# A streaming encoder step on one core: both feed-forwards begin with two blocks taken by quarter

## The chip, the cores and the metric

The kernel runs on one core of one Trainium2 chip. The metric is device time in microseconds (us). Before the change three runs took 2466.3, 2466.51 and 2468.87, with the median at 2466.51.

A core has five engines with queues of their own: PE (TensorE: products and transposes; its weight loads are listed as PEld), DVE (VectorE), ACT (ScalarE), POOL (GpSimd) and SP (SyncE, which here issues most loads and stores). Engines wait for one another by semaphores. Products accumulate in banks of the PSUM memory (512 columns of f32 each), which VectorE and ScalarE read.

## The reference

One step of a macaron encoder: half a SwiGLU feed-forward, an in-projection, attention and a recurrence side by side, a gated merge, an out-projection, half a feed-forward, and a last norm. All activations and weights are f32, D = 1024, D_FF = 2816.

```
def half_ffn(x, g, w_gate, w_up, w_down):
    h = rmsnorm(x, g)
    return x + 0.5 * ((silu(h @ w_gate) * (h @ w_up)) @ w_down)

x = half_ffn(x, ffn1_norm, ffn1_w_gate, ffn1_w_up, ffn1_w_down)
qa, ka, va, zf, ih, qh, g, ga, gb = split(rmsnorm(x, mix_norm) @ w_in)
...
merged = sigmoid(ga + b) * (oa @ w_branch_a) + sigmoid(gb + b) * (ob @ w_branch_b)
x = x + merged @ w_out
x = half_ffn(x, ffn2_norm, ffn2_w_gate, ffn2_w_up, ffn2_w_down)
y = rmsnorm(x, final_norm)
```

oa is the stick-breaking attention's output, ob that of the HGRN2 recurrence. There are 1072 token columns: 16 meta tokens, 1024 prompt frames and 32 sample frames. The outputs are y, the new K and V rows and the recurrence's states.

## The kernel before

**Layout.** Activations lie feature-major: 128 features on the partitions, 8 k-tiles for D, token columns along the free dimension. An f32 operand is split in a high and a low half (ScalarE copies the high one, VectorE subtracts to get the low one, `split` at L219 and L220; `weights` does it for a loaded block at L202 and L203). A product of one k-tile is three matmuls: high by high, high by low, low by high (L103 in the profile, where every matmul is recorded; transposes are L106). A product of four k-tiles by 268 columns is thus 12 matmuls, called a half product below.

**Feed-forwards.** The columns are cut in four quarters of 268 (264 in FFN2), two halves `b` by two halves `th`. Blocks of 128 hidden features come in units of two. The class `Seven` computes each unit by a seven-product scheme (Strassen) on 2 by 2 blocks of operands; the scheme needs the sums T1 to T4 of operand quarters, which `sums(b)` makes on VectorE. Blocks 0 and 1 are not done in this way: `plain` takes them as ordinary products, so that PE has work while the operands and sums are made. Before, `plain(0)` goes over all four quarters for the gate and the up weights of block 0, then `plain(1)` for block 1; `rest` follows with units 1 to 10. Their results go through `mid_dram` to the down projection, a list of jobs of seven products p1 to p7 that `run` interleaves: p6 and p7 of a job stand inside the next job.

**FFN1's start.** The token rows are loaded in row tiles of 128 (`xt`) with leftovers of 12 rows per quarter (`odds`). For a quarter, ScalarE takes square sums, a chain of small VectorE operations and one POOL power gives the row scales (L790 to L796), POOL writes them on a diagonal (L804, L807), PE spreads them over the partitions by a product with ones, ScalarE copies that to `R`, and `columns` turns the rows by transposes, scales them (L836) and splits them. All rows are asked for ahead of the weights. The sums of both halves stand between `plain(0)` and `plain(1)`.

**Merge.** `merge(m)` for block m loads two gates (`ga`, `gb`, L1633), multiplies the two branch products by them (L1641) and splits the sum into `mh`, `ml`. `out_block` adds out-projections into `acc`, which starts as the residual (three loads, L1624, issued ahead of the first gates). The blocks go in groups (0, 1), (2, 3), (4) and (5, 6, 7); the last group goes over three column tiles of 384, 384 and 288, and behind each tile `squares` takes its square sums (L1661, L1662), a product with ones adds them up, and `operands` scales and splits the tile for FFN2 (L1693).

**What sets the order.** A scheduler orders each engine's instructions from their dependences, except where `PE.on` keeps PE in the order of the code, and where a dependence is added by hand. `bank(rotate=True)` hands out PSUM banks in turn; the tags are mm, z, tr and o.

Of the kernel before, what the change touches and what calls it, by code (L numbers as in the profile page):

```python
# [82 lines left out]
def tile_encoder_step(ctx, tc, x_prompt, x_sample, cache_k, cache_v, state_hgrn, meta_tokens,  # L83
# [101 lines left out]
    def weights(parts, own=None):  # L185
        raw = wp.tile([P, D], F32, tag="raw", name="raw", bufs=2)
        n = 0
        for src, k in parts:
# [13 lines left out]
        A.activation(hi, raw, AF.Copy)  # L202
        V.tensor_tensor(lo, raw, hi.bitcast(F32), op=ALU.subtract)  # L203
# [14 lines left out]
    def split(dst_h, dst_l, src):  # L218
        A.activation(dst_h, src, AF.Copy)  # L219
        V.tensor_tensor(dst_l, src, dst_h.bitcast(F32), op=ALU.subtract)  # L220
# [50 lines left out]

    def finish_one():
        while waiting:
            waiting.pop(0)()
# [54 lines left out]
    class Seven:  # L329
# [60 lines left out]
        def plain(self, c, before=lambda q: None, after=lambda q: None):  # L390

            qw, where = self.qw, self.where
            gw = self.ahead.pop(c) if c in self.ahead else self.block(self.w_gate, c)
            uw = self.block(self.w_up, c)
            g = self.tile("g", [P, T])
            for q in range(4):
                before(q)
                b, th = divmod(q, 2)
                pss = []
                for wh, wl in (gw, uw):  # L400
                    ps = bank(rotate=True)
                    for kh in range(2):
                        ks = slice(kh * 512, (kh + 1) * 512)
                        product(ps, (wh[:, ks], wl[:, ks]), self.B[kh, th, b], kh == 0)
                    pss.append(ps)
                after(q)
                silu(where(g, th, b), pss[0][:, :qw])
                V.tensor_tensor(where(g, th, b), pss[1][:, :qw], where(g, th, b), op=ALU.mult)
            self.gs.append(g)
# [164 lines left out]
        def down(self, w, resid, final, after, early):  # L574
# [70 lines left out]
            def run(jobs):  # L645
# [9 lines left out]
                for job in jobs:  # L655
                    step(job.p1)
                    if before:
                        step(before.p6)
                    step(job.p2)
                    step(job.p4 if job.done == "end" else job.p3)  # L660
                    if before:
                        step(before.p7)
                        if before.done:
                            queue += before.done()
                            every[0] = max(1, 20 // len(queue))
                    step(job.p3 if job.done == "end" else job.p4)
                    if job.done == "end":
# [3 lines left out]
                if before.done != "end":  # L671
                    before.p6()
                before.p7()
# [68 lines left out]
    with tc.tile_pool(name="f1", bufs=2) as pool:  # L742
# [21 lines left out]
        G.memset(odds, 0.0)  # L764
        rows = []
        for q in range(4):
            for h in range(2):
                tag, n = (("g", 4), ("g", 4), ("raw2", 2), ("S", 2))[q]
                xt = pool.tile([P, D], F32, tag=tag, name="xt", bufs=n)
                load(xt, 0, q * QW + h * P, P)  # L770
                rows.append(xt)
            if q == 0:
                for x in range(4):
                    load(odds, 32 * x, x * QW + 2 * P, ODD)
# [3 lines left out]
        functions("silu_and_others")  # L778

        def scales(tiles):  # L780
            m = len(tiles)
            ss = pool.tile([P, 3, 4], F32, tag="ss", name="ss", bufs=4)
            V.memset(ss, 1.0)
            for j, xt in enumerate(tiles):
                for h in range(2):
                    junk = temp(pool, "junk")
                    A.activation(junk.bitcast(BF16)[:, :512], xt[:, h * 512:(h + 1) * 512], AF.Square,
                                 accum_out=ss[:, h, j:j + 1])
            ms, y, r1 = ss[:, 0, :m], ss[:, 1, :m], ss[:, 2, :m]
            V.tensor_tensor(ms, ms, y, op=ALU.add)  # L790
            V.tensor_scalar(ms, ms, 1.0 / D, EPS, op0=ALU.mult, op1=ALU.add)
# [1064 lines left out]
```

## Time and profile before

| | us |
|---|---|
| median of three runs | 2466.51 |
| the profiled execution | 2468.0 |
| its span in the profile | 2466.2 |
| PE busy | 2396.0 |
| VectorE busy | 1669.0 |
| ScalarE busy | 1017.8 |
| POOL busy | 257.1 |

The span is the profiled execution from its first to its last instruction. A group of instructions is given as line, engine, operation, output <- input, then the count; `[... <-X]` is the idle time ahead of an instruction and who ended it. The name of the output is that of the tile in the code: `ps_z` is a bank with the tag z. PEclk is the clock granted to TensorE, 1.00 being full. PE's busy time includes stretches at half of it.

### The profile page before, as it was taken

What the parts mean: (1) busy time and instruction counts of PE and PEld (TensorE: products, weight loads), DVE (VectorE), ACT (ScalarE), POOL (GpSimd) and SP (SyncE); (2) the same over time, 40 slices, a digit from 0 to 9 for tenths busy, and PEclk for the clock granted to TensorE, in tenths of its full rate; (3) what the DMA queues carried; (4) which work ended last, traced back from release to release, by engine and by line L of the source; (5) the groups of instructions that cost most, each with busy time, mean ns of one, the idle gap of its engine ahead of it and who ended that gap; (6) DMA issues with size and microseconds to landing.
All of it is one profiled execution on the core that took longest, in us unless ns stands there. A gap on an engine that the chain in (4) does not pass through costs nothing.

```text
span 2466.2 us, 47916 instructions
## 1 busy us (share of the span) xinstructions
PE 2396.0 (97%) x19500; PEld 2292.9 (93%) x19500; DVE 1669.0 (68%) x3144; ACT 1017.8 (41%) x2129; POOL 257.1 (10%) x461
## 2 busy tenths in 40 slices
PE   6999999999999999999999999999799999999997
PEld 5999999989999998899888888999799999999997
DVE  4866676767766477764666665556966767676876
ACT  6444444442225233332445544323444444453223
POOL 1011010100003012121000000112011111110000
PEclk9999999999999999999999999999899999999999
DMA  7334343487652111111211122522234444468761
GB/s 199 106 127 164 124 168 123 160 315 280 244 211 79 50 44 48 57 48 50 59 45 45 49 67 62 193 87 100 75 130 150 140 150 141 152 239 323 272 237 72
DMA packets 270371, 331.93 MB, mean 135 GB/s; under 512 B 41078, under 2 KB 228726, under 8 KB 264518
## 3 DMA queue, kind: packets, MB, share of 16 engines
q1 hardware_dynamic: 247942, 244.96, 29.7%
q0 software_dynamic: 22208, 83.91, 9.0%
q8 instruction: 153, 2.51, 0.4%
q14 instruction: 68, 0.56, 0.1%
HBM read 213.93 MB, written 114.89 MB: 133 GB/s over the span
## 4 chain that ended last, share of the span: by engine, by line
PE 84%; DVE 5%; issue 5%; DMA 4%; ACT 2%; POOL 1%; SPq 0%; DVEq 0%; ACTq 0%; POOLq 0%
PE ps_mm L103 28%; PE ps_z L103 26%; PE ps_o L103 9%; PE pu L103 6%; PE ps_tr L103 5%; PE pf L103 4%; PE pv L103 4%; PE ps_tr L106 2%; DMA mid_dram<-st 1%; DMA raw<-in_ffn_w_down_dram 1%; PE ps_z L106 1%; DMA u_xl<-mid_dram 1%; DVE wlo L203 1%; POOL mid_dram L371 1%; PE ps_mm L106 0%
## 5 line engine op out<-in xcount | busy, mean ns | idle before, releaser
L103 PE MATMUL ps_mm<-xh,whi 128*128 128x384 f32 (+2 forms) x960 | 320.0, 334 | 0.5 <-DVE raw L1487 0.5
L103 PE MATMUL ps_mm<-xh,wlo 128*128 128x384 f32 (+2 forms) x960 | 313.2, 326 | 0.0
L103 PE MATMUL ps_mm<-xl,whi 128*128 128x384 f32 (+2 forms) x960 | 312.8, 326 | 0.0
L219 ACT ACTIVATE whi<-S 128x1024 fp32r<-128x1024 f32 x122 | 129.3, 1059 | 311.3 <-PE ps_z L103 135.7
L371 POOL DMA_DIRECT2D mid_dram<-st x150 | 104.3, 706 | 830.4 <-DVE st L220 805.5
L103 PEld LDWEIGHTS ps_mm<-xh,whi 128*128 128x128 f32 x960 | 181.1, 189 | 9.1 <-issue 5.0
L103 PEld LDWEIGHTS ps_mm<-xl,whi 128*128 128x128 f32 x960 | 181.0, 189 | 1.2
L103 PEld LDWEIGHTS ps_mm<-xh,wlo 128*128 128x128 f32 x960 | 181.2, 189 | 0.3
L220 DVE TENSOR_TENSOR wlo<-S,whi 128x1024 fp32r<-128x1024 f32 x122 | 149.1, 1222 | 34.3 <-ACT whi L219 31.4
L220 DVE TENSOR_TENSOR st<-g,st 128x536 fp32r<-128x536 f32 (+1 forms) x150 | 104.7, 710 | 85.8 <-ACT st L219 85.8
L202 ACT ACTIVATE whi<-raw 128x1024 fp32r<-128x1024 f32 x67 | 70.4, 1056 | 180.9 <-PE ps_mm L103 139.1
L1279 DVE TENSOR_TENSOR_SCAN left<-left,oneb 128x512 f32<-128x512 f32 (+6 forms) x112 | 107.4, 959 | 54.8 <-ACT left L119 54.2
L220 DVE TENSOR_TENSOR wlo<-raw,whi 128x1024 fp32r<-128x1024 f32 x80 | 76.6, 957 | 75.4 <-ACT whi L219 73.6
L219 ACT ACTIVATE st<-g 128x536 fp32r<-128x536 f32 (+1 forms) x150 | 94.5, 643 | 79.4 <-DMA mid_dram<-st 63.8
L103 PE MATMUL ps_z<-acc1s,whi 128*128 128x268 f32 (+1 forms) x480 | 106.3, 285 | 0.0
L103 PE MATMUL ps_z<-xh1s,whi 128*128 128x268 f32 (+1 forms) x360 | 102.8, 286 | 0.0
L103 PE MATMUL ps_z<-xl1s,whi 128*128 128x268 f32 (+1 forms) x360 | 102.6, 285 | 0.0
L103 PE MATMUL ps_z<-xh1s,wlo 128*128 128x268 f32 (+1 forms) x360 | 102.6, 285 | 0.0
L103 PE MATMUL ps_z<-xh2s,whi 128*128 128x268 f32 (+1 forms) x352 | 100.4, 285 | 0.0
L103 PE MATMUL ps_z<-xl2s,whi 128*128 128x268 f32 (+1 forms) x352 | 100.3, 285 | 0.0
L103 PE MATMUL ps_z<-xh2s,wlo 128*128 128x268 f32 (+1 forms) x352 | 100.1, 285 | 0.0
L203 DVE TENSOR_TENSOR wlo<-raw,whi 128x1024 fp32r<-128x1024 f32 x67 | 82.8, 1241 | 25.1 <-ACT whi L202 21.3
(715 smaller groups left out, 7603.8 us busy)
## 6 DMA issues: line engine op xcount, KB each, us to landing
mid_dram<-st POOLq DMA_DIRECT2D x75, 536.0 KB, 3.9
mid_dram<-st POOLq DMA_DIRECT2D x75, 528.0 KB, 4.0
raw<-in_ffn_w_gate_dram SPq DMA_DIRECT2D x44, 512.0 KB, 3.7
raw<-in_ffn_w_up_dram SPq DMA_DIRECT2D x44, 512.0 KB, 3.8
raw<-in_w_in_dram SPq DMA_DIRECT2D x44, 512.0 KB, 3.7
raw<-in_ffn_w_down_dram SPq DMA_DIRECT2D x40, 512.0 KB, 6.1
u_xl<-mid_dram SPq DMA_DIRECT2D x8, 1608.0 KB, 6.6
u_xh<-mid_dram SPq DMA_DIRECT2D x8, 1608.0 KB, 10.8
```

The lines of the kernel that those rows point to most:

```text
L103: return self.queue(nc.tensor.matmul(*args, **more))
L106: return self.queue(nc.tensor.transpose(*args, **more))
L202: A.activation(hi, raw, AF.Copy)
L203: V.tensor_tensor(lo, raw, hi.bitcast(F32), op=ALU.subtract)
L219: A.activation(dst_h, src, AF.Copy)
L220: V.tensor_tensor(dst_l, src, dst_h.bitcast(F32), op=ALU.subtract)
L371: nc.gpsimd.dma_start(self.mids[i, :, :, NAMES.index(name)], st.bitcast(F32))
L1279: V.tensor_tensor_scan(rev(st[:rows]), rev(st[:rows]), one, 1.0 if carry is None else carry[:rows], op0=ALU.mult, op1=ALU.mult)
```

## The change

1. *FFN1's start.* The leftovers follow the first two row tiles, then four weight blocks (gate and up of blocks 0 and 1), then the other rows. Products of a zero tile `busy` are put ahead of the first transposes (18), ahead of the first spread (6) and ahead of the first real product (5). A square sum is one operation over 1024 columns. The first quarter's scale chain and diagonal are VectorE's alone but for the power; the later ones are POOL's. `first_columns` turns seven k-tiles into seven banks at once and splits them two at a time.
2. *`plain((0, 1))`.* Both blocks together, quarter by quarter: four fixed banks (mm, mm, tr, o) take gate and up of blocks 0 and 1, first for the lower four k-tiles, then for the upper four. After each half product a callback `step(q, j)` may put in work for the next quarter (transposes, spread) and the sums, which now stand inside quarters 1 and 3. The same in FFN2.
3. `lmax` and `causalb` on VectorE are held back behind a mark.
4. *Merge's start.* `merge` is now the class `Merge`. One residual tile is loaded ahead of the gates of blocks 0 and 1, two behind them.
5. *Out-projections.* The groups are (0, 1), (2, 3), (4, 5); inside a tile four banks take one block after another.
6. *Merge's end.* Blocks 6 and 7 go tile by tile: both merge products of tile j, then the product with ones and the scaling for tile j - 1, then the out-projection of tile j, then its square sums. `operands` is a list of pieces which are put in one at a time, between out-projections of tile 1 and inside FFN2's first quarters.
7. *Down projections.* One job more (`tight`) has all of its seven products done before the next job begins.

PE at the merge's end, around the product with ones (`cst`) that adds up the square sums of the second column tile (`t_ga` before, `ga` and `gb` after); `mh` and `ml` are a merged block's halves, `whi`, `wlo` and `raw_...` those of weights, `xh_17813` the branch outputs of the third tile. Before:

```order
L103 MATMUL ps_mm<-mh,raw_19293 128x288
L103 MATMUL ps_mm<-ml,raw_19293 128x288
L103 MATMUL ps_mm<-mh,raw_19294 128x288
L103 MATMUL ps_z<-t_ga,cst 128x384 x2
L103 MATMUL ps_tr<-mh,whi 128x288
L103 MATMUL ps_tr<-ml,whi 128x288
L103 MATMUL ps_tr<-mh,wlo 128x288
```

After:

```order
L103 MATMUL ps_o<-mh,raw_19174 128x384
L103 MATMUL ps_o<-ml,raw_19174 128x384
L103 MATMUL ps_o<-mh,raw_19175 128x384
L103 MATMUL ps_z<-xh_17813,whi 128x288
...
L103 MATMUL ps_mm<-xh_17813,wlo 128x288
L103 MATMUL ps_z<-ga,cst 128x384
L103 MATMUL ps_z<-gb,cst 128x384
L103 MATMUL ps_z<-mh,whi 128x288
L103 MATMUL ps_z<-ml,whi 128x288
```

Before, the product with ones follows three out-projections of the third tile; after, the 48 matmuls of the third tile's merge products (those of `xh_17813`) stand ahead of it, behind the second tile's out-projections.

VectorE in FFN1's second quarter, after the change (L873 scales a k-tile, L930 to L933 are the sums, L229 the splits' low halves, L411 the multiply of gate and up that empties an up bank):

```order
L229 TENSOR_TENSOR xl1s<-acc0s,xh1s 128x1072
L411 TENSOR_TENSOR g<-ps_o,g 128x268
L873 SCALAR_TENSOR_TENSOR acc0s<-ps_z,gains,R 128x268 x4
L931 TENSOR_TENSOR S<-acc0s,S 128x1072
L932 TENSOR_TENSOR s<-xe_137,S 128x1072
L229 TENSOR_TENSOR xl0s<-acc0s,xh0s 128x1072
L933 TENSOR_TENSOR s<-acc0s 128x1072
L229 TENSOR_TENSOR xl1s<-s,xh1s 128x1072
L411 TENSOR_TENSOR g<-ps_mm,g 128x268
```

The sums, which had stood behind all quarters of block 0, are now between the scalings and the multiplies of one quarter.

SP at the merge's start, before (`acc` the residual tiles, `ga` and `gb` the gates):

```order
L1624 DMA acc_17867<-x_dram 128x8x384
L1624 DMA acc_17868<-x_dram 128x8x384
L1624 DMA acc_17869<-x_dram 128x8x288
L1633 DMA ga<-gate_dram 128x1056
L1633 DMA gb<-gate_dram 128x1056
```

and after:

```order
L1725 DMA acc_17868<-x_dram 128x8x384
L1736 DMA ga<-gate_dram 128x1056
L1736 DMA gb<-gate_dram 128x1056
L1736 DMA ga<-gate_dram 128x1056
L1736 DMA gb<-gate_dram 128x1056
L1725 DMA acc_17869<-x_dram 128x8x384
L1725 DMA acc_17870<-x_dram 128x8x288
```

Four gate loads have moved ahead of the second and the third residual tile.

The diff, cut to what the parts above speak of:

```diff
-        def plain(self, c, before=lambda q: None, after=lambda q: None):
+        def plain(self, cs, step=lambda q, j: None, tags=(None,) * 2):
...
             for q in range(4):
-                before(q)
                 b, th = divmod(q, 2)
-                pss = []
-                for wh, wl in (gw, uw):
-                    ps = bank(rotate=True)
-                    for kh in range(2):
-                        ks = slice(kh * 512, (kh + 1) * 512)
-                        product(ps, (wh[:, ks], wl[:, ks]), self.B[kh, th, b], kh == 0)
-                    pss.append(ps)
-                after(q)
-                silu(where(g, th, b), pss[0][:, :qw])
-                V.tensor_tensor(where(g, th, b), pss[1][:, :qw], where(g, th, b), op=ALU.mult)
+                pss = [bank(tag, tag is None) for tag in tags]
+                for kh in range(2):
+                    ks = slice(kh * 512, (kh + 1) * 512)
+                    for j, (wh, wl) in enumerate(x for c in cs for x in ws[c]):
+                        product(pss[j], (wh[:, ks], wl[:, ks]), self.B[kh, th, b], kh == 0)
+                        to = where(gs[cs[j // 2]], th, b)
+                        if kh and j % 2 == 0:
+                            silu(to, pss[j][:, :qw])
+                        elif kh:
+                            V.tensor_tensor(to, pss[j][:, :qw], to, op=ALU.mult)
+                        step(q, kh * len(pss) + j)
...
+                    tight = job.done in ("end", "tight")
...
+                    if tight:
+                        step(job.p7)
+                        before = None
...
+                        if s == last - 2 and mp == 3:
+                            job.done = "tight"
...
+        row_tiles(0)
+        for x in range(4):
+            load(odds, 32 * x, x * QW + 2 * P, ODD)
+        raw_weights(0)
+        raw_weights(1)
+        for q in range(1, 4):
+            row_tiles(q)
...
+        def warm(n, ps):
+            for _ in range(n):
+                PE.matmul(ps, busy[:, :P], busy[:, P:P + 512], start=True, stop=True)
...
+        def first_columns():
+            x0s = [f32s("s") for _ in range(2)]
+            pss = [bank(tag) for tag in ("mm", "mm", "tr", "o", "z", "z", "z")]
+            warm(18, pss[-1])
+            for k in range(KC - 1):
+                turn(0, k, pss[k], (0,))
...
+            spread(0, 6)
...
+            warm(5, bank("mm"))
...
-        ff.plain(0, columns_ahead)
-        t4s = [sums(b) for b in range(2)]
-        ff.plain(1)
+        def step(q, j):
+            if (q, j) == (0, 1):
+                first_rest()
+            if q < 3:
+                if j == 3:
+                    spread(q + 1)
+                    if q < 2:
+                        diagonal(q + 2, scales(rows[2 * q + 4:2 * q + 6], G, latest[0]), odd, G)
+                elif j == 5:
+                    columns(q + 1, 0)
+            if q and j == 0:
+                columns(q, 1)
+            if (q, j) in ((1, 5), (3, 1)):
+                sums(q // 2)
+
+        ff.plain((0, 1), step, ("mm", "mm", "tr", "o"))
...
+        for m in range(6):
+            mids[m] = Merge(m)
+            if m == 1:
+                residual()
+            for t in TD:
+                mids[m].tile(*t)
             if m in (2, 4):
-                out_block((m - 2, m - 1), [mids.pop(m - 2), mids.pop(m - 1)], False)
+                out_block((m - 2, m - 1), [mids.pop(m - 2), mids.pop(m - 1)])
+        out_block((4, 5), [mids.pop(4), mids.pop(5)])
+        u6, u7 = Merge(6), Merge(7)
...
+        for j, (t0, n) in enumerate(TD):
+            for u in (u6, u7):
+                u.tile(t0, n)
+            kept(j)
+            if j:
+                finish()
+                todo += operands(*TD[j - 1])
...
+            for ms in (range(4), range(4, KC)):
+                for m in one(ws, (u6, u7), ms, slice(t0, t0 + n)):
...
+            finish = squares(t0, n, u6.g + u7.g)
```

More of the change, by code (lines that the diff above doesn't have):

```diff
@@ L183, in tile_encoder_step, with planned, weights @@
     big = Wide
-    def weights(parts, own=None):
-        raw = wp.tile([P, D], F32, tag="raw", name="raw", bufs=2)
+    def planned(made, last):
+        tc.add_manual_dep(made.ins, last.ins.name, order, reason="order")
+    def weights(parts, own=None, raw=None, behind=None, later=None):
         n = 0
+        if raw is None:
+            raw = wp.tile([P, D], F32, tag="raw", name="raw", bufs=2)
         for src, k in parts:
@@ new lines, in columns @@
+        def columns(q, kh):
+            b, th = divmod(q, 2)
+            x0 = pool.tile([P, 4, QW], F32, tag="g", name="x0", bufs=4) if q == 2 else f32s("s")
+            v = value(kh, th, b)
+            for k in range(4):
+                ps = bank("z")
+                turn(q, 4 * kh + k, ps, range(3))
+                of = scaled(q, 4 * kh + k, ps, v[:, k])
+                planned(A.activation(x0[:, k], ps[:, :QW], AF.Copy), of)
+            nc.sync.dma_start(x0_dram[:, 4 * kh:4 * kh + 4, q * QW:(q + 1) * QW], x0)
+            split(*B[kh, th, b], v)
@@ new lines, in sums @@
+            split(*X["T3", b], t3)
+            X["T4", b] = B[0, 1, b]
+            X["B11", b], X["B21", b], X["B22", b] = B[0, 0, b], B[1, 0, b], B[1, 1, b]
+            if b == 0:
+                split(*X["T4", b], t4)
+            else:
+                ff.t4 = t4
+        PE.on = True
+        r = scales([rows[0], odds, rows[1]], V)
+        odd = r[1]
+        wsq = [weights([], None, raws[0][0], latest[0], diagonal(0, [r[0], r[2]], odd, V))]
+        first_rest = first_columns()
+        diagonal(1, scales(rows[2:4], G, latest[0]), odd, G)
@@ L882, in tile_encoder_step @@
+        ff.plain((0, 1), step, ("mm", "mm", "tr", "o"))
+        PE.on, PE.last = False, None
+        split(*X["T4", 1], ff.t4)
         constants()
[L883 to L886 removed]
         ff.rest()
@@ L1782, in tile_encoder_step @@
-        ff.plain(0, after=lambda q: finish_one())
+        ws = [out_weights(6), out_weights(7, ff.spare)]
+        finish, todo = None, []
+        for j, (t0, n) in enumerate(TD):
[5 more added lines that the diff above has]
+                todo += operands(*TD[j - 1])
+            if j == 2:
+                own = [ff.tile("g", [P, D], F32R) for _ in range(2)]
+                ff.ahead[0] = [ff.block(w, 0) for w in (ffn2_w_gate, ffn2_w_up)]
+                ff.ahead[1] = [ff.block(ffn2_w_gate, 1),
+                               weights([(ffn2_w_up[0][:, P:2 * P], KC)], lambda: own)]
+            for ms in (range(4), range(4, KC)):
+                for m in one(ws, (u6, u7), ms, slice(t0, t0 + n)):
+                    if m % 2:
+                        nc.sync.dma_start(x2_dram[:, m - 1:m + 1, t0:t0 + n], acc[:, m - 1:m + 1, t0:t0 + n])
+                        if j == 1 and len(todo) > 2:
+                            todo.pop(0)()
+            finish = squares(t0, n, u6.g + u7.g)
@@ L1783, in tile_encoder_step, with step @@
+        t4s = []
+        def step(q, j):
+            if (q, j) == (0, 3):
+                finish()
+                todo.extend(operands(*TD[2]))
+            elif todo and j != 2:
+                todo.pop(0)()
+            if (q, j) in ((2, 2), (3, 2)):
+                t4s.append(sums(q - 2))
+        ff.plain((0, 1), step, ("mm", "mm", "tr", "o"))
         PE.on, PE.last = False, None
-        t4s = [sums(b) for b in range(2)]
-        ff.plain(1)
         for b in range(2):
```

329 lines of the change are left out of this document (168 added, 161 removed).

## The prediction

> **What bounds the kernel now.** I read the page from the top: busy times, granted clock, then the chain of work that ended last.
>
> ```profile
> span 2466.2 us, 47916 instructions
> PE 2396.0 (97%) x19500; PEld 2292.9 (93%) x19500; DVE 1669.0 (68%) x3144; ACT 1017.8 (41%) x2129; POOL 257.1 (10%) x461
> PEclk9999999999999999999999999999899999999999
> PE 84%; DVE 5%; issue 5%; DMA 4%; ACT 2%; POOL 1%; SPq 0%; DVEq 0%; ACTq 0%; POOLq 0%
> ```
>
> TensorE is busy for 97% of the span, so only 70 us are left in which it does nothing, plus what it loses where its clock is halved. The change adds no useful product and removes none, so whatever it gains is in those two places. The waits of PE, longest in total first, say where the idle time lies; a row gives the waiting tile, the releaser, the total, the count and the longest.
>
> ```profile
> PE ps_z L106 <- DMA xt<-in_x_prompt_dram: 7.0, 2, 6.3
> PE ps_mm L103 <- DVE wlo L203: 6.4, 1, 6.4
> PE ps_z L103 <- DVE t_ga L1662: 6.0, 1, 6.0
> PE ps_mm L103 <- POOL t_ys L804: 5.7, 1, 5.7
> PE ps_z L103 <- POOL t_ys L804: 3.8, 1, 3.8
> PE ps_mm L103 <- DVE acc0s L836: 2.8, 1, 2.8
> PE pv L103 <- DMA u_xl<-mid_dram: 2.3, 2, 1.7
> PE ps_z L103 <- DVE ga L1641: 1.9, 1, 1.9
> ```
>
> These eight rows are four places: FFN1's start (L106, L804, L836), merge's start (L1641), the passage from the merge to FFN2 (L1662, L203), and the waits for FFN tiles in the down projections. The change touches all four, each of which I price apart.
>
> **FFN1's start.** First the chain before, in order of time (start, length, what), and the rows from which its head is built: ScalarE's square sums of the first two row tiles, the leftovers' transposes, VectorE's ends of the scale chain, one scaling, one split, two low halves of weights, and the loads of the first 24 us.
>
> ```profile
> 35.41 5.73 PE ps_mm L103 x24
> 44.99 0.53 PE ps_z L106 x3
> 66.43 2.96 PE ps_mm L103 x24
> 93.14 2.97 PE ps_z L103 x24
> ```
>
> ```profile
> 6.26 0.63 ACT L787 ACTIVATE t_ms<-xt 128x512 bf16<-128x512 f32 x1 [2.95 <-DMA xt<-in_x_prompt_dram]
> 8.51 0.63 ACT L787 ACTIVATE t_ms<-xt 128x512 bf16<-128x512 f32 x1 [0.78 <-DMA xt<-in_x_prompt_dram]
> 9.95 0.38 PE L106 MATMUL ps_z<-cst,odds 12*128 12x12 f32 x2
> 13.47 0.16 DVE L790 TENSOR_TENSOR ss<-ss 128x3 f32<-128x3 f32 x1 [10.08 <-ACT t_ms L787]
> 15.52 0.16 DVE L796 TENSOR_TENSOR ss<-ss 128x3 f32<-128x3 f32 x1
> 18.83 0.50 DVE L836 SCALAR_TENSOR_TENSOR acc0s<-ps_z,gains,R 128x268 f32<-128x268 f32 x1 [1.82 <-ACT R L809]
> 22.90 1.28 DVE L220 TENSOR_TENSOR xl0s<-acc0s,xh0s 128x1072 fp32r<-128x1072 f32 x1 [0.32 <-ACT xh0s L219]
> 32.59 2.36 DVE L203 TENSOR_TENSOR wlo<-raw,whi 128x1024 fp32r<-128x1024 f32 x2
> 44.06 0.93 PE L103 MATMUL ps_tr<-t_ys,cst 128*128 128x128 f32 x6
> raw<-in_ffn_w_up_dram SPq DMA_DIRECT2D x1, 512.0 KB, 11.2
> DMA packets 4565, 6.66 MB, mean 277 GB/s; under 512 B 307, under 2 KB 3493, under 8 KB 4565
> ```
>
> Before, the first real product starts at 35.41 and the last plain one ends at 93.14 + 2.97 = 96.1. In between lie 16 products of 2.96 = 47.4, 16 turned k-tiles of 0.53 = 8.5, two spreads of 0.93, and 5.73 - 2.96 = 2.8 of half clock: 60.5, so PE hardly waits there. Everything to be won stands ahead of 35.41.
>
> After, the rows of a quarter are needed sooner and fewer. Row tiles land at 6.2 and 8.4 as before and the leftovers by 9.9. A square sum is one operation of 1024: about 1.2 from the 0.63 for 512, so the third ends near 11.8. The scale chain took 15.68 - 13.47 = 2.2 less one addition, 2.05: 13.9. The diagonal (three small VectorE operations beside 0.16 to 0.50, I take 0.6) gives 14.5, the spread at full clock 0.93, its copy 0.4: the scalings begin at 15.9. Two scalings and the half split behind them, then one more VectorE step, make the first product **17.6**. The weights would be there: the first row tile, the second, the leftovers, the constants and four blocks are 3.5 MB, landed by 14.5 at 277 GB/s behind the first 2 us, where before the second block landed at 10.56 + 11.2 = 21.7. The ends are 15.9 (the scalings themselves) and 22 (the weights as late as before).
>
> From there the PE work is the 47.4 again, now 24 + 1 turned k-tiles (13.2) and three spreads (2.8): 63.4. The 29 dummy products on a zero tile are in the wait for rows or for scalings, where PE has nothing; if that cover went they would cost at most 29 x 0.2 = 6, by a 512-column product at the rate of 2.96 for 24 of 268. To this come waits, because the first quarter is tight on VectorE: 8 scalings of 0.5, 4 half splits of 0.64, 4 low halves of 1.18, 4 multiplies of 0.5 make 13.3, and PE's 8 half products with spread and one turn are 13.3 too. VectorE starts first and feeds, so PE runs behind it: I take 4.5 of waiting there, 1.5 in the later quarters (their VectorE load is 4.0 + 2.6 + 2.0 = 8.6, with 10.2 of sums in two of them, against 17.0 of PE), and 0.6 for half a chance of one more stretch at half clock. Together 17.6 + 63.4 + 6.6 = 87.6 against 96.1: **-8.5**, from -15 (no waits) to 0 (first product at 22, and 10 of waiting).
>
> The holding back of lmax and causalb, and POOL's scale chains and diagonals for quarters 1 to 3, are costed at nothing: a quarter's 17 us of PE cover them, and without that cover each quarter would pay the 2.05 of a chain once more.
>
> **Merge's start.** SP's issues, then PE.
>
> ```profile
> 1542.21 10.77 SPq L1624 DMA_DIRECT2D acc<-x_dram  x3
> 1553.20 0.47 SPq L1633 DMA_DIRECT2D ga<-gate_dram  x1
> 1562.72 0.44 PE L103 MATMUL ps_z<-xh,whi 128*128 128x384 f32 x1 [1.90 <-DVE ga L1641]
> 1564.08 0.52 PE L103 MATMUL ps_z<-xh,whi 128*128 128x384 f32 x1
> 1564.40 0.52 PE L103 MATMUL ps_z<-xl,whi 128*128 128x384 f32 x1
> ```
>
> SP sits 10.77 us on the three residual loads, and the gates' load is queued behind them. PE waits 1.90 for a multiply that needs a gate. Then the starts lie 0.32 apart (1564.08, 1564.40) where a 384-column product at full clock takes 2.96/24 x 384/268 = 0.18; over 3.4 us that loses 1.7. With one residual tile ahead instead of three, the gates leave some 7 us sooner (two thirds of 10.77), and both terms go: **-3.6**. Moved behind the gates are two residual loads and SP's later weight loads; they are needed by the first out-projection, two merge blocks later. The ends are -3.6 and 0, where the gates' tiles themselves are held.
>
> Here the Trainium skill speaks, on its page "TensorE: Matmul & The Clock Gate", section "HAM oscillation — how this bites in real kernels": only PE-idle gaps above some 3.4 us bring the slow clock back. By that rule this term would be -1.9 and the new short waits below would be free; the trace shows a half clock after 1.90 idle, and I keep the row's price.
>
> **Merge to FFN2.** PE's two waits, one of VectorE's operations there, and stretches: their bounds and length, the busy time of PE, its weight loads, VectorE, ScalarE and POOL, then the granted clock and the DMA's share and rate.
>
> ```profile
> 1736.04 1.65 PE L103 MATMUL ps_z<-t_ga,cst 128*128 128x384 f32 x2 [6.04 <-DVE t_ga L1662]
> 1754.88 0.59 PE L103 MATMUL ps_mm<-xh0s,wlo 128*128 128x264 f32 x1 [6.44 <-DVE wlo L203]
> 1733.30 0.56 DVE L1755 TENSOR_TENSOR acc<-ps_z,acc 128x384 f32<-128x384 f32 x1
> 1727.50:1755.00 27.50, 15.02 (x90) 13.58 (x89) 23.50 (x55) 13.70 (x23) 2.39 (x3) 0.81 0.33 111
> 1738.00:1740.00 2.00, 2.00 (x10) 2.00 (x10) 0.55 (x2) 1.36 (x3) 0.00 (x0) 0.50 0.00 0
> 1755.00:1757.00 2.00, 2.00 (x9) 2.00 (x10) 2.00 (x5) 0.54 (x1) 0.00 (x0) 0.50 0.39 112
> 1785.00:1800.00 15.00, 15.00 (x126) 15.00 (x125) 8.26 (x14) 4.11 (x6) 2.11 (x3) 1.00 0.47 163
> ```
>
> In 27.5 us PE is busy 15.02 and VectorE 23.50; the waits are 6.04 + 6.44 and each is followed by a stretch at clock 0.50 (about 3.4 us, of which PE is busy in 5.0 and 3.3: half of that, 2.5 and 1.65, is lost). All four together are 16.6. The change moves the merge products of blocks 6 and 7 into this stretch: for tiles 1 and 2 that is 48 x 0.18 + 48 x 0.13 = 14.9 of PE, enough to fill both holes. They bring VectorE 12 operations of 0.4 to 0.56, about 6. So VectorE has 23.5 + 6 = 29.5 and PE 27.5 - 16.6 + 14.9 = 25.8: VectorE is short by up to 3.7 unless work runs over the stretch's end, where FFN2's first quarters now want half the operands at a time. I take 2.4 of new waits: **-14.2**. The ends are -16.6, and -8 if one of the two holes comes back with its half clock.
>
> **Tight job.** The FFN tiles u that PE waits 2.3 for in all are freed by a product of the job before. In the order after, that job's last two products run 2 x 2.96 = 5.9 us sooner, above the longest wait of 1.7. **-2.3**, and 0 if the load and not the tile is late.
>
> **Sum.** -8.5 - 3.6 - 14.2 - 2.3 = -28.6. The profiled execution took 2468.0 (span 2466.2), so 2439.4; it stands 1.5 above the median of 2466.51, which gives **2438**.
>
> **The rivals.**
> - *VectorE becomes the bound in the quarters.* For it: 13.3 against 13.3 in the first quarter and 29.5 against 25.8 at FFN2. Against it: from 1785 on VectorE is busy only 8.26 of 15.00, so a backlog can drain. Three more us in the first quarter and 1.5 in each of three later ones (7.5), FFN2 at -8.3: -1.0 - 3.6 - 8.3 - 2.3 = -15.2, so 2451. Chance 0.25.
> - *Slower: four fixed banks.* A quarter's next product needs the bank that VectorE's multiply of the last one has to empty; behind a block of sums (8 operations of 1.28, 10.2) that multiply is late by 10.2 less the three products ahead of it (3 x 1.48 = 4.4), 5.8. In the four quarters with sums beside it that is 23 and the time 2461; it becomes slower from 3.6 per quarter in all eight, and at 5.8 in all eight it is 2466.5 - 28.6 + 46 = 2484. Against it: only four quarters have sums. Chance 0.04.
> - *It does not do what it says.* The weights land at 22, SP's gates wait for their tiles, the u loads are late by themselves: -4.1 - 14.2 = -18.3, 2448. Chance 0.12.
> - *The clock falls again.* Every wait that leaves PE about half idle for 3.4 us costs another 1.7. Four such: 2445. Chance 0.10.
>
> **How the numbers follow.** The forecast keeps 0.49. Its own bounds, all terms at their good end (-15 - 3.6 - 16.6 - 2.3), would give 2429; I reach to 2430 below, and above to 2454, past the VectorE rival's 2451 and short of its tail and the banks. 0.2% is 5 us, about what a measurement of this kernel can tell from no change. Within it (2461.6 to 2471.4) end the tail of the VectorE case and the banks at their lower price, 0.05; slower by more 0.03; faster 0.92.
>
> **What would show it.** First real product near 17.6 and the first split of the next unit near 88; fewer than 7 us of PE waits between. No wait for a gate at merge's start, and clock 1.00 there. No wait above 2 us at the merge's end. No wait for u in the down projections. I am wrong if the chain shows VectorE between the quarters' products, or PE waiting for a bank that a multiply of g empties.

## The result and the profile after

The changed kernel takes 2455.8 us (median of six runs, 2451.32 to 2460.32) against 2466.41 before (six runs, 2465.03 to 2471.39): a ratio of 0.9948, with a 95% interval of 0.9938 to 0.9958. It is faster by 10.6 us, where 28.5 had been forecast, and lies above the range's end of 2454. Its own runs lie in two groups, 2451 to 2453 and 2458 to 2460; the profiled execution is the fastest, 2451.32 with a span of 2449.5, so its trace shows the change at its best and not at its median.

The head of the page and the chain of work that ended last:

```profile
span 2449.5 us, 47940 instructions
PE 2401.2 (98%) x19529; PEld 2291.2 (94%) x19529; DVE 1669.4 (68%) x3131; ACT 1014.9 (41%) x2110; POOL 267.6 (11%) x472
PE 69%; issue 16%; DVE 7%; DMA 4%; POOL 2%; ACT 2%; DVEq 0%; SPq 0%; POOLq 0%; ACTq 0%
```

PE is busy 5 us longer than before in a span that is 16.7 shorter; the 29 dummies (the products of the zero tile) are in that number, and so are products at half clock. The largest of PE's waits that stand where those of before stood, or are new (waiting tile, releaser, total, count, longest):

```profile
PE ps_mm L103 <- DVE acc L1858: 3.2, 2, 1.8
PE ps_z L103 <- DVE gb L1768: 2.6, 1, 2.6
PE ps_z L103 <- DVE half L802: 2.4, 1, 2.4
PE pv L103 <- DMA u_xl<-mid_dram: 1.2, 2, 0.8
PE ps_mm L103 <- DVE xl2s L229: 1.2, 1, 1.2
PE ps_mm L103 <- DVE acc0s L873: 1.0, 1, 1.0
```

Of the eight rows of before, those for rows, for a gate and for the low half of a weight at the merge's end are gone. The others fell: the scaling in FFN1's start from 2.8 to 1.0 (L873), the scale chain there from 9.5 to 0.8 (L835, not shown), the product with ones at the merge's end from 6.0 to 2.6 (L1768), the loads of u from 2.3 to 1.2. The row of `half` is the start of the program, ahead of the first dummy, and that of `xl2s` stands in FFN1's last quarter. L1858 is new: there PE waits at the start of FFN2 for a bank that an addition of the out-projection has to empty.

From each trace the starts of the same products were read, and the differences give the length of a stage. "Head" is from the start of the program to the first product of unit 1 of FFN1; "projection, attention" from the first in-projection product to the last one of the attention; "merge's start" from there to the first out-projection; "merge's end" from there to the first product of unit 1 of FFN2. The end is the start of PE's last product. The column "again" is a second profile of the same changed kernel, from a run of 2462.17.

| stage, us | before | after | again |
|---|---|---|---|
| head | 95.93 | 89.36 | 89.82 |
| FFN1's units | 417.96 | 417.73 | 417.94 |
| first down projection | 231.66 | 230.32 | 232.57 |
| projection, attention | 801.48 | 800.87 | 805.32 |
| merge's start | 36.34 | 33.20 | 35.87 |
| merge's end | 218.07 | 213.23 | 212.27 |
| FFN2's units | 409.19 | 408.87 | 410.23 |
| second down projection | 244.41 | 244.77 | 245.20 |
| end | 2455.04 | 2438.35 | 2449.23 |

Against before, the first profile has -6.6 at the head, -1.3 in the first down projection, -3.1 at the merge's start and -4.8 at its end. The second has the head and the merge's end too, and gives back 3.8 in a stage that the change does not touch.

### The profile page after: what moved, and what is told of

Same layout as the page of the kernel before. It is cut to its first block, busy times and chain, and to the rows that moved or that the text cites. A ratio compares the mean times of both kernels' runs of the same rounds, so it can differ in the third digit from the quotient of the medians.

```text
span 2449.5 us, 47940 instructions
## 1 busy us (share of the span) xinstructions
PE 2401.2 (98%) x19529; PEld 2291.2 (94%) x19529; DVE 1669.4 (68%) x3131; ACT 1014.9 (41%) x2110; POOL 267.6 (11%) x472
## 4 chain that ended last, share of the span: by engine, by line
PE 69%; issue 16%; DVE 7%; DMA 4%; POOL 2%; ACT 2%; DVEq 0%; SPq 0%; POOLq 0%; ACTq 0%
PE ps_mm L103 24%; PE ps_z L103 18%; PE ps_o L103 7%; PE pu L103 6%; PE ps_tr L103 4%; PE pf L103 4%; PE pv L103 3%; POOL mid_dram L376 2%; PE ps_tr L106 2%; DMA mid_dram<-st 1%; PE ps_z L106 1%; DMA u_xl<-mid_dram 1%; DMA raw<-in_ffn_w_down_dram 1%; DVE wlo L210 1%; ACT whi L207 0%
## 5 line engine op out<-in xcount | busy, mean ns | idle before, releaser
L103 PE MATMUL ps_mm<-xh,whi 128*128 128x384 f32 (+2 forms) x976 | 325.0, 333 | 0.5 <-DVE raw L1586 0.5
L229 DVE TENSOR_TENSOR wlo<-S,whi 128x1024 fp32r<-128x1024 f32 x122 | 149.2, 1223 | 29.9 <-ACT whi L228 27.0
L229 DVE TENSOR_TENSOR st<-g,st 128x536 fp32r<-128x536 f32 (+1 forms) x150 | 104.6, 710 | 74.8 <-ACT st L228 74.7
L207 ACT ACTIVATE whi<-raw 128x1024 fp32r<-128x1024 f32 x65 | 68.5, 1056 | 170.7 <-PE ps_mm L103 136.2
L229 DVE TENSOR_TENSOR wlo<-raw,whi 128x1024 fp32r<-128x1024 f32 x80 | 76.6, 957 | 75.7 <-ACT whi L228 73.9
L228 ACT ACTIVATE whi<-raw 128x1024 fp32r<-128x1024 f32 x80 | 67.6, 845 | 70.4 <-PE ps_z L103 35.3
L103 PE MATMUL ps_z<-xe,whi 128*128 128x264 f32 (+1 forms) x400 | 82.9, 284 | 0.1
L119 ACT ACTIVATE g<-g 128x268 f32<-128x268 f32 (+1 forms) x120 | 49.6, 420 | 60.2 <-DVE g L453 60.2
L103 PE MATMUL pv<-u_xl,g 128*128 128x268 f32 (+1 forms) x420 | 70.5, 285 | 1.2 <-DMA u_xl<-mid_dram 1.2
L1380 DVE TENSOR_TENSOR aa<-aa,left 128x512 f32<-128x512 f32 (+6 forms) x112 | 61.5, 549 | 13.6
L228 ACT ACTIVATE g<-raw 128x256 fp32r<-128x256 f32 x120 | 41.8, 408 | 68.8 <-PE pf L103 61.0
L103 PE MATMUL ps_z<-xh1s,whi 128*128 128x268 f32 (+1 forms) x240 | 68.8, 287 | 0.0
```

Source lines behind the costliest of these rows:

```text
L103: return self.queue(nc.tensor.matmul(*args, **more))
L119: i = A.activation(out, in_, func, **more).ins
L207: made = A.activation(hi, raw, AF.Copy)
L228: return (A.activation(dst_h, src, AF.Copy), V.tensor_tensor(dst_l, src, dst_h.bitcast(F32), op=ALU.subtract))
L1380: V.tensor_tensor(at[:rows, :n], at[:rows, :n], left[:rows, 513 - n:], op=ALU.mult)
```

## The experiments

Each kernel was timed against the kernel before on the same chip; the ratios are to before, with their 95% intervals.

| kernel | median, us | before, us | ratio | interval |
|---|---|---|---|---|
| ff1_only | 2470.48 | 2467.97 | 1.0009 | 1.0000 to 1.0018 |
| merge_only | 2456.41 | 2467.97 | 0.9955 | 0.9943 to 0.9968 |
| no_tight | 2461.62 | 2467.97 | 0.9969 | 0.9956 to 0.9981 |
| after_again | 2456.38 | 2467.97 | 0.9952 | 0.9938 to 0.9965 |
| rot4 | 2449.56 | 2468.99 | 0.9922 | 0.9909 to 0.9934 |
| before_rot4 | 2470.72 | 2468.99 | 1.0008 | 0.9999 to 1.0017 |
| ff1_rot4 | 2468.45 | 2468.99 | 0.9997 | 0.9988 to 1.0006 |
| mid_finish | 2447.31 | 2468.99 | 0.9912 | 0.9898 to 0.9925 |
| ff1_rot4_tight | 2462.07 | 2468.27 | 0.9977 | 0.9967 to 0.9987 |
| before_tight | 2466.76 | 2468.27 | 0.9990 | 0.9981 to 0.9998 |
| warm_end | 2450.77 | 2468.27 | 0.9930 | 0.9917 to 0.9943 |
| no_dummies | 2447.51 | 2468.27 | 0.9917 | 0.9905 to 0.9930 |

### The parts alone

ff1_only is the kernel before with FFN1's start of the change; merge_only has the merge and FFN2's start and not the rest; no_tight is the changed kernel without the tight job; after_again is the changed kernel. The edits are the change's own, cut at the pool of FFN1 and at that of FFN2; no_tight is

```diff
-                        if s == last - 2 and mp == 3:
-                            job.done = "tight"
```

> The kernel before with the change's FFN1 start alone (row and weight order, dummies, quarters, sums inside). Theory A (the parts add up, and the missing gain is at the merge's end): about 6.5 us faster than before, as the start of unit 1 moved from 95.9 to 89.4 in the profiles, and runs as close together as those of before. Rival B (the FFN1 quarters are what varies from run to run, by stretches at half clock behind their short waits): 0 to 6 us faster, with a spread of some 7 us among the runs. The prediction's term was 8.5.

> The kernel before with the change's merge and FFN2 start alone (no FFN1 quarters, no tight job). Theory A: 8.6 us faster (3.7 at the merge's start, 4.8 at its end, by the profiles). Rival B, if the spread between runs comes from here: 2 to 9 us faster with runs some 7 us apart. The prediction's terms were 3.6 + 14.2 = 17.8.

> The changed kernel without the tight job. By the profiles the tight job brought 1.35 in the first down projection and nothing clear in the second: 1 to 2 us slower than the changed kernel, so about 9 us faster than before. If the tight job was worth the predicted 2.3, 8 faster; if it disturbs the second projection, as fast as the changed kernel or faster.

> The changed kernel itself once more, for a second profile and more runs. Theory A and B both: median near 2456, runs from 2451 to 2460 in two groups; if the groups come from the clock, the slower group shows a granted clock of 0.993 where the faster shows 0.995.

merge_only brings 11.6 us by itself, as much as the whole change. ff1_only brings nothing: 2.5 slower, though its head ends at 89.83 in the profile, 6.1 sooner than before. So theory A fell for FFN1 and rival B was not it either: the quarters are as fast as in the changed kernel, and the gain is lost later, in ff1_only's profile 3.8 in the attention's stage, 1.3 and 3.0 in the two down projections and 1.1 in FFN1's units. no_tight is 5.2 slower than the changed kernel in the median, against a predicted term of 2.3; the runs of both spread widely (2455.55 to 2462.08, and 2453.23 to 2462.17), so the size is uncertain. Two of after_again's five runs, 2455.81 and 2456.38, lie between the two groups of the first six.

The loss in the attention's stage shows in the second profile of the changed kernel too, in a view of stretches (bounds, length, busy time of PE, weight loads, VectorE, ScalarE, POOL, granted clock, DMA share and rate):

```profile
1530.00:1534.00 4.00, 4.00 (x46) 3.40 (x45) 2.98 (x7) 2.79 (x7) 0.00 (x0) 1.00 0.10 37
1534.00:1538.00 4.00, 4.00 (x26) 3.33 (x24) 2.07 (x6) 1.04 (x3) 0.00 (x0) 0.58 0.05 8
1538.00:1542.00 4.00, 4.00 (x24) 3.48 (x24) 1.02 (x3) 0.44 (x1) 0.00 (x0) 0.50 0.99 351
1542.00:1546.00 4.00, 4.00 (x28) 3.31 (x27) 0.12 (x2) 0.00 (x0) 0.00 (x0) 0.50 0.11 38
1546.00:1550.00 4.00, 4.00 (x13) 4.00 (x14) 4.00 (x11) 0.45 (x1) 0.00 (x0) 0.50 0.70 233
```

PE is busy in every one of these 4.00 and waits for nothing, and its clock is 0.50 from 1534.7 to 1551.7. ff1_only and no_tight show the same stretch; before and merge_only do not. What PE runs there are the attention's last products, of 16 or 32 rows by 32 columns, between products of the in-projection. PE's timeline just ahead of the stretch, first of before, then of the second profile after:

```profile
1537.06 0.86 PE L103 MATMUL ps_o<-aT,vc 16*64 16x32 f32 x10
1537.85 0.45 PE L103 MATMUL ps_mm<-xh,whi 128*128 128x384 f32 x1
1538.13 0.34 PE L103 MATMUL ps_mm<-xl,whi 128*128 128x384 f32 x1
1538.31 0.34 PE L103 MATMUL ps_mm<-xh,wlo 128*128 128x384 f32 x1
1538.49 0.51 PE L103 MATMUL ps_mm<-xh,whi 128*128 128x384 f32 x2
1538.93 0.30 PE L103 MATMUL ps_o<-aT,vs 32*64 32x32 f32 x2
```

```profile
1531.60 0.86 PE L103 MATMUL ps_o<-aT,vc 16*64 16x32 f32 x10
1532.39 0.57 PE L103 MATMUL ps_mm<-xh,whi 128*128 128x288 f32 x2
1532.89 0.30 PE L103 MATMUL ps_o<-aT,vs 32*64 32x32 f32 x2
```

Before, five products of the in-projection stand between two rows of 24 small ones; after, two, one of 288 columns and one of 384 (a row gives the shape of its first). Nobody changed that stage. But `bank(rotate=True)` hands out banks in a turn of eight, FFN1's start took 52 of them before (spread, columns and `plain`) and takes none now, so the turn arrives at the in-projection moved by 52 mod 8 = 4, and the scheduler fills the gaps of the attention with other products.

### The turn of the banks put back

rot4 is the changed kernel with one line more, behind FFN1's first blocks; ff1_rot4 is ff1_only with the same line; before_rot4 puts that line into the kernel before, behind its `plain(1)`:

```diff
         PE.on, PE.last = False, None
+        rot[0] += 4
```

> The changed kernel with the turn of the PSUM banks moved on by four behind FFN1's first blocks, as it stood there before the change; in PE's order this puts five products of the in-projection (not two) between two rows of small attention products near 1530 us. Theory C (the slower clock there is a side effect of that order): no stretch at half clock from 1533 to 1550, the slower group of runs gone, median near 2452 (14 to 16 us below before). Rival P (the stretch comes by the phase of the clock's windows, whatever the order): median stays near 2456 with the same two groups.

> The kernel before, with nothing but the turn of the banks moved on by four behind FFN1's first blocks, so that PE's order near 1530 us becomes that of the changed kernel (two products, not five). Theory C: slower than before by 4 to 7 us in most runs, with half clock from about 1540 to 1555. Rival P: no difference.

> The change's FFN1 start alone with the turn of the banks put back. Theory C: 4 to 6.5 us faster than before (2462 to 2464), where ff1_only was 2.5 slower. Rival Q (FFN1's quarters themselves cost the clock): no faster than 2468.

rot4's runs are 2448.68 to 2451.3, one group, and the median is 6.8 below after_again (which ran on another chip; by the ratios to before, 0.9922 against 0.9952). PE's order has the five products again, and the clock stays, here in rot4's stretches of the same bounds:

```profile
1534.00:1538.00 4.00, 4.00 (x43) 3.35 (x43) 2.07 (x6) 1.11 (x3) 0.00 (x0) 1.00 0.00 0
1538.00:1542.00 4.00, 4.00 (x43) 3.51 (x43) 1.23 (x4) 0.45 (x1) 0.00 (x0) 1.00 0.98 328
```

The attention is not the only place that the turn reaches: the merge's end takes 207.97 in rot4's profile, and 213.23 and 212.27 in those of the changed kernel. There the last out-projections sit in the banks z, mm, z, mm, and FFN2's first two half products, whose tags are fixed as mm and mm, wait for VectorE's additions to empty them. The additions and the first matmuls of the waiting half products in the changed kernel (start, length, what):

```profile
1732.80 0.45 DVE L1858 TENSOR_TENSOR acc<-ps_mm,acc 128x288 f32<-128x288 f32 x1
1733.30 0.39 PE L103 MATMUL ps_mm<-xh0s,whi 128*128 128x264 f32 x1 [1.43 <-DVE acc L1858]
1736.32 0.44 DVE L1858 TENSOR_TENSOR acc<-ps_mm,acc 128x288 f32<-128x288 f32 x1
1736.82 0.39 PE L103 MATMUL ps_mm<-xh0s,whi 128*128 128x264 f32 x1 [1.79 <-DVE acc L1858]
```

With the turn put back the last banks are z, tr, z, o, and the first of these half products starts without a wait:

```profile
1733.59 0.28 PE L103 MATMUL ps_mm<-xh0s,whi 128*128 128x264 f32 x1
```

merge_only, where nothing moved the turn, does not have these waits either; after_again and no_tight have them, 3.2 and 4.1 in all. So rot4's gain is that of two places, and its 6.8 is not the price of the attention's stretch alone.

The order in the attention separates the profiles. Nine have the five products, and none shows the stretch; five have the two (the two of the changed kernel, ff1_only, no_tight and before_rot4), and all but the first of the changed kernel show it. before_rot4 shows it in a kernel that has nothing else of the change:

```profile
1540.00:1544.00 4.00, 4.00 (x23) 3.11 (x21) 1.65 (x5) 0.93 (x2) 0.00 (x0) 0.50 0.43 122
1544.00:1548.00 4.00, 4.00 (x23) 3.37 (x23) 1.13 (x3) 0.44 (x1) 0.00 (x0) 0.50 0.74 271
```

Its projection and attention take 805.43, with 801.48 before. In time it is 1.7 slower in the median, not 4 to 7: its runs reach from 2466.0 to 2475.8, six of eleven above 2470.5, so the order opens the way to the stretch and does not force it; the changed kernel's profiled run had the order and escaped. That part of rival P stands.

ff1_rot4 missed its expectation: 2468.45, no gain, with the clock at 1.00 in the attention. Its stages are 89.91 at the head (6.0 sooner), and then 235.09 and 246.55 in the down projections (3.4 and 2.1 longer than before). The waits there in ff1_rot4, then in the same kernel with the tight job:

```profile
PE pv L103 <- ACT pu L649: 4.0, 2, 2.5
PE pv L103 <- DMA u_xl<-mid_dram: 3.7, 2, 1.8
```

```profile
PE pv L103 <- ACT pu L649: 2.3, 1, 2.3
PE pv L103 <- DMA u_xl<-mid_dram: 0.9, 2, 0.5
```

### The tight job with and without the new head

ff1_rot4_tight and before_tight are ff1_rot4 and the kernel before, each with the tight job's lines of the change.

> ff1_rot4 with the tight job. In the profile of ff1_rot4 the 6.0 us won at FFN1's start were lost again, 3.0 in the first down projection and 3.4 in the second, by waits for its tiles u. Theory F (the head lets the down projections' loads collide, and the tight job is what keeps the gain): 4 to 7 us faster than before (2462 to 2465). Rival G (they are lost by chance of the clock's windows, wherever): within 2 us of ff1_rot4, no faster than 2466.

> The kernel before with the tight job alone. The prediction's term was 2.3 (both waits for u gone). Theory F, where the job is worth more with the new head than without: 1 to 2.5 us faster than before. Rival G: the 5 us between the changed kernel and no_tight again, whatever the head.

With the new head the job is worth 6.4 us (2468.45 to 2462.07), without it 1.5. In time theory F holds. Its mechanism is shown in part. In the second projection the wait for a load of u grows with the new head from 0.64 before to 1.81 (ff1_rot4), 2.0 (no_tight) and 2.1 (ff1_only), and the job brings it to 0.45. In the first one it does not grow: 1.67 before, then 1.85, 1.7 and 1.1. The job brings it to 0.49 there. That is 2.7 of the 6.2 us by which the job shortens the two projections in these profiles (235.09 to 231.40, 246.55 to 244.00); the rest is for the most part a wait for ScalarE of 1.5 and half clock behind waits, and both come and go from profile to profile. Why the load comes later in the second projection is not shown: PE's and SP's orders there are those of before, and SP issues it 180.3 us into the stage before and 181.3 in ff1_rot4. It stays open.

### The merge's end

In the changed kernel VectorE holds up the second product with ones. PE first, then VectorE ahead of it (start, length, what):

```profile
1721.39 1.01 PE L103 MATMUL ps_z<-gb,cst 128*128 128x384 f32 x1 [2.64 <-DVE gb L1768]
```

```profile
1709.10 3.07 DVE L1793 SCALAR_TENSOR_TENSOR acc<-acc,gains,R 128x264 f32<-128x264 f32 x4
1712.56 0.88 DVE L1793 SCALAR_TENSOR_TENSOR acc<-acc,gains,R 128x264 f32<-128x264 f32 x2
1713.37 1.25 DVE L229 TENSOR_TENSOR xl0s<-acc,xh0s 128x1056 fp32r<-128x1056 f32 x1
1714.54 1.64 DVE L1793 SCALAR_TENSOR_TENSOR acc<-acc,gains,R 128x264 f32<-128x264 f32 x2
1717.50 1.24 DVE L229 TENSOR_TENSOR xl0s<-acc,xh0s 128x1056 fp32r<-128x1056 f32 x1
1720.80 0.54 DVE L1768 TENSOR_TENSOR gb<-gb 128x384 f32<-128x384 f32 x1
```

From 1709 to 1719 some 8 us of the first tile's scalings and splits run among the second tile's additions, and the last square sum ends at 1721.34. They run so late because the first tile's scale R comes late: its product with ones stands behind the merge products of both blocks, while VectorE has gaps of 0.9 to 2.05. mid_finish moves it:

```diff
             for u in (u6, u7):
                 u.tile(t0, n)
+                if j == 1 and u is u6:
+                    finish()
             kept(j)
             if j:
-                finish()
+                if j == 2:
+                    finish()
                 todo += operands(*TD[j - 1])
```

> rot4, and in the merge's second tile the product with ones and the scaling of the first tile stand between the two merge blocks instead of behind both. Theory D (VectorE has the first tile's operands ahead of the second tile's square sums because they come too late): operands begin some 4 us sooner, the wait of 2.64 at the second product with ones goes and with it a stretch at half clock: 4 to 6 us faster than rot4. Rival E (that wait is POOL's or ScalarE's): same as rot4, within 1.5 us.

The wait is gone, and the product with ones follows PE's own work:

```profile
1719.74 0.29 PE L103 MATMUL ps_o<-xh,wlo 128*128 128x288 f32 x1
1719.87 0.81 PE L103 MATMUL ps_z<-ga,cst 128*128 128x384 f32 x2
1720.51 0.81 PE L103 MATMUL ps_z<-gb,cst 128*128 128x384 f32 x2
```

So that wait was VectorE's, as theory D says. The time fell by 2.3, from 2449.56 to 2447.31, less than the 4 to 6 expected, and with intervals that overlap. The stage went from 207.97 in rot4 to 206.93 only, and no_dummies below, with the same code in this stage as rot4, has 209.39. The idle time did not go, it moved: PE is idle for 4.3 us of the stage in rot4 and for 4.3 in mid_finish. These are its waits there:

```profile
PE ps_z L103 <- ACT mh L228: 1.8, 3, 1.1
PE ps_tr L103 <- ACT gb L1765: 1.4, 1, 1.4
PE ps_z L103 <- DVE ml L229: 1.1, 3, 0.8
```

In the second tile the out-projections now want the second block before its split is done (1.1), and another wait, of 1.4, stands at the start of FFN2. The median is the lowest of the study, with no_dummies 0.2 above it.

warm_end asks what the clock alone is worth there: 12 products of constants, written to a bank that nobody reads, fill the wait in rot4.

```diff
+                if j == 2:
+                    warm2(12)
                 finish()
```

> rot4 with 12 products of constants, written to a bank nobody reads, ahead of the second product with ones at the merge's end, where PE waited 2.64 in rot4 and two stretches at reduced clock followed. Theory H (the clock falls because PE does too little in a window): no half clock between 1720 and 1732, about 2 us faster than rot4 though nothing is done sooner. Rival I (the clock falls for another reason, or the dummies come on top): same or up to 2.6 us slower.

The stretch of the wait and that behind it, and the start of FFN2, in rot4 and then in warm_end:

```profile
1720.00:1724.00 4.00, 1.45 (x9) 0.84 (x7) 4.00 (x9) 3.66 (x7) 0.35 (x1) 1.00 0.52 197
1724.00:1728.00 4.00, 3.38 (x11) 2.47 (x12) 3.57 (x8) 2.29 (x5) 1.49 (x2) 0.67 0.01 2
```

```profile
1720.00:1724.00 4.00, 3.95 (x26) 2.87 (x26) 4.00 (x8) 3.51 (x6) 0.00 (x0) 1.00 0.26 98
1724.00:1728.00 4.00, 3.36 (x14) 1.65 (x12) 3.57 (x8) 2.61 (x6) 1.83 (x2) 1.00 0.26 100
1736.00:1740.00 4.00, 1.43 (x12) 1.25 (x11) 3.82 (x6) 2.11 (x5) 2.42 (x2) 1.00 0.80 228
1740.00:1744.00 4.00, 4.00 (x22) 4.00 (x21) 3.51 (x11) 1.82 (x4) 0.00 (x0) 0.57 1.05 309
```

With the dummies the clock stays at 1.00 behind the wait, as theory H has it. It brings no time: 2450.77 against 2449.56. In warm_end PE is busy 1.43 in the stretch from 1736, with VectorE at 3.82 of 4.00, and the half clock comes there instead. So the clock does not set the length of this stage. PE's wait there, 2.6, is put down to a square on ScalarE that itself waits for an addition on VectorE. But that VectorE's load is the bound is not shown: ahead of these additions it stands idle for 1.16 itself, for a copy of a weight on ScalarE, which had waited 1.88 for its load.

### FFN1's dummies

no_dummies is rot4 with `range(0)` for `range(n)` in `warm`.

> rot4 without the 29 products of the zero tile in FFN1's head. If they keep the clock up: the transposes, the spread and the first products run at half clock until about 24 us, the first unit starts 2 to 3 us later than in rot4 (89.7), and the time is 2 to 3 us above rot4's 2449.6. Rival (they do nothing, since two of the profiles show half clock from 10 to 23 in spite of them): within 1 us of rot4.

Its head does run at half rate until 23.4, by the lengths of its products (0.43 and then 0.28; the clock row shows 1.00 there), and its unit 1 starts at 90.37, 0.7 later than in rot4, not 2 to 3. The time is 2447.51, 2.0 below rot4, with intervals that overlap: the dummies bring nothing that these runs can tell. They do not keep the clock either: rot4's is 0.50 from 11.9 to 22.1 in spite of them. The changed kernel's first profile has its products at full rate from 18.9 on, and its unit 1 starts at 89.36, 0.3 before rot4's. PE's clock matters little there, as at the merge's end.

## Why the prediction was wrong

Four steps failed, in the order of the kernel: FFN1's start was too large and needs the tight job, the tight job was priced alone, a moved turn of the banks was not in the sum at all, and the merge's end, the largest miss, was priced from VectorE's total load, with no wait for a bank and no half clock behind the new waits.

**FFN1's start: right in kind, too large by a quarter, and not worth its number by itself.** The first product was set at 17.6 and came at 17.92. From there to 89.36 is 71.4, where 70.0 had been set, 63.4 of work, 6.0 of waits and 0.6 for the clock. PE's waits in it are 4.8, so the work was the part set too low: 66.7. The term was -8.5; of nine profiles with the new head and the dummies of the change, eight have the head between 89.30 and 89.91, -6.0 to -6.6, and warm_end at 90.90. What the sum did not have is that the gain needs the tight job: ff1_rot4 loses it all in the down projections, ff1_rot4_tight keeps 6.2 of both together.

**Merge's start: right, in part by luck.** The term was -3.6, 1.9 of wait and 1.7 of half clock. With the old order in the attention it is 32.63 against 36.34, -3.7, in merge_only, rot4 and mid_finish alike, and no wait for a gate is left. But ff1_rot4 and ff1_rot4_tight, whose merge is that of before, take 34.58 and 34.64: the wait is there (1.68 and 1.73), and no half clock follows it. So 1.7 of the term hangs on where a half-clock stretch falls in the kernel that it is compared with. In the profiles with the stretch at half clock it is smaller, 35.87 in after_again, because that stretch runs into it.

**Merge's end: the term that was mis-sized most.** It was -14.2, 16.6 less 2.4 of new waits, with nothing for the clock. Measured are -4.8 and -5.8 (the changed kernel), -8.5 (merge_only) and -10.1 (rot4). In the changed kernel's first profile PE is idle for 6.5 us of the stage, 4.1 more than was set, and its clock is 0.50 for 10.2 us, which costs an estimated 5; -14.2 with these two is -5. The idle time has two causes.
- The wait of 2.64 comes from the order on VectorE. The sum had VectorE short by 3.7 (29.5 against 25.8) and put 2.4 of that on PE, as if its backlog would drain behind FFN2's start. But the square sums of the second tile, which PE's next product with ones wants, stood behind the first tile's operands, whose scale arrives late. The wait was priced from the total load of a stretch where it hangs on the order within it. mid_finish shows this: with the order changed the wait is gone. It shows too that other waits take its place.
- The waits of 1.43 and 1.79 are for banks, and come from the moved turn. The rival of the four fixed banks had priced such waits inside the quarters, behind the multiplies of g, where they did not come; it did not see the out-projections ahead of FFN2.

The prediction calls the half-clock stretches of before about 3.4 us long. In the trace they are 6.8 each, with 5.0 and 3.3 of PE's work in them, and its price goes by the latter.

**Tight job: mis-sized, because it was priced alone.** The term was -2.3. Alone it is 1.5 (before_tight); with the new head 6.4 (ff1_rot4 against ff1_rot4_tight), and 5.2 by the less certain pair of no_tight and after_again. The wait for u does not go to 0 with it either: 1.2 is left in the changed kernel.

**The term that was missing: the turn of the banks.** The prediction took every stage outside its four places as unchanged. The excerpts of the order at three places were right, but a counter of banks couples FFN1's start with the in-projection some 1440 us later, and with the banks at the start of FFN2. rot4 gains 6.8 by putting it back. The clock rival spoke of falls behind a wait that leaves PE half idle; the stretch in the attention came with PE busy all the time, so that rival had the kind of loss and not the place.

**The rules of the clock.** The prediction kept the row's half clock after 1.90 of idle, against the rule that it cites. before and before_tight (1.87) have it there, and so has the wait of 2.64 at the merge's end; behind the 1.68 and 1.73 of ff1_rot4 and ff1_rot4_tight it did not come. So a wait of this length can bring the half clock and need not. The Trainium skill's page "TensorE: Matmul & The Clock Gate", section "What's actually happening", says that the clock follows how busy the PE has been recently. Where dummies fill the wait (warm_end, 1.00 against rot4's 0.67) the trace agrees; in the stretch at 1538 the row has PE busy in 4.00 of 4.00 and a clock of 0.50, so if the clock follows how busy PE is, it does not go by busy time as the profile counts it.

With the turn of the banks put back, 19.4 us of the 28.6 are there (2468.99 to 2449.56). In rot4's profile the head is 2.2 short of its term and the merge's end 4.1, and the two down projections, for which -2.3 was set, take 476.6 against 476.1 before. The in-projection with the attention and FFN2's units move by 1 to 2 us from profile to profile.

## What to carry to other kernels

A change that takes something from a rotating resource (banks, buffers) moves every later user of it, here a stage that was not rewritten and the banks that a rewritten one wants first; the order of every stage should be compared, and one line that puts the turn back is a cheap test. Where an engine is nearly full, price the wait for it from the order of its work up to the releasing instruction, not from its total load; look for the wait that comes next when one is taken away, and do not expect a warmer clock on the waiting engine to gain. Terms that shift the same loads are not independent: measure each alone and together.

## What was not expected of the hardware

In a stage of products with 16 or 32 rows and 32 columns of moving data TensorE's clock was 0.50 for 13.6 to 17.1 us (four profiles) while the profile shows PE fully busy. It came only where two products of 288 and 384 columns, and not five, stood among some fifty small ones, and even then not every time: the changed kernel's first profile, 2451.32, has the order and not the stretch. The first six runs of that kernel, three from 2451 to 2453 and three from 2458 to 2460, fit this, though only one of them has a trace. Why the clock falls there is not shown.

On POOL, operations on two numbers a partition took up to 1.06 us, where VectorE's took 0.16 before:

```profile
24.47 1.03 POOL L824 TENSOR_TENSOR ss<-ss 128x2 f32<-128x2 f32 x1
25.58 1.06 POOL L825 TENSOR_TENSOR ss<-ss 128x2 f32<-128x2 f32 x1
27.35 0.20 POOL L827 TENSOR_TENSOR ss<-ss 128x2 f32<-128x2 f32 x1
```

The same kind of operation took 0.20 in the same chain; what the longer ones waited for inside is not shown, and the profile's spans on POOL are rough.
